# A hybrid decoder layer on one core: the gating unit's two projections as one with 512 columns, and 128 bytes more ahead of two groups of tiles

## The chip, the core and the metric

The kernel runs on one core of one Trainium2 chip. It uses the five engines: PE (TensorE, matrix products; PEld is its weight load), DVE (VectorE), ACT (ScalarE), POOL (GpSimd) and SP (SyncE, which issues the DMAs). The metric is device time in microseconds from launch to end, median over runs.

## The reference, cut to what matters

One layer, 1024 tokens of width 1024, float32. The part that the change touches is the fourth of four mixers, a gating unit over chunks of 128 tokens:

```python
h = rmsnorm(x, ln1_g) * (1 + sc1) + sh1
(..., d_u, d_v) = split(h @ w_in, splits, axis=-1)        # 256 columns each
# sgu_mixer(d_u, d_v)
u = gelu(u)
v = layernorm(gelu(v), ln_g, ln_b)                        # over the 256 columns
sv = einsum('gts,bnsge->bntge', w_causal, v.chunks(128)) + b_s
o_d = u * sv
mix = concat([o_a, o_b, o_c, o_d]) @ w_out
x = x + g1 * mix
x = x + g2 * conv_ffn(rmsnorm(x, ln2_g) * (1 + sc2) + sh2, ffn_up, ..., ffn_down)
```

Ahead of `w_out` stand a convolution with a LayerNorm (`o_a`), gated linear attention (`o_b`) and a dilated attention (`o_c`); `conv_ffn` is an up-projection to 5632 columns, a causal convolution of width 3 and a down-projection from 2816.

## The kernel before, in words

Every float32 product is made of three products with operands rounded to a shorter format. A tile is split into a high part (`ac.copy`, line 70) and a low part (a subtraction on POOL or DVE, line 71), and low times high, high times low and high times high are added up in PSUM (lines 92 to 94, and 1221 to 1223 in the second half of the kernel). The activations of the first half stand in 32 tiles `h` of 128x512 (high and low, by 8 slices of the width and 2 token halves).

The first half goes stage by stage: `first` and `proj_feat` and `proj_tok` project `h` onto groups of columns of `w_in`, one after the other. `weave(main, (gen, rate), ...)` advances the generators of the other mixers some steps at each step of the main projection: attention (`att`), convolution norm (`cn`), linear attention (`lin`), the sums for the later modulations (`ada`, line 828 on DVE) and the splits of finished mixers (`sp`). The tile framework then orders the instructions of each engine by a simulated time line; each engine runs its own in order.

Weights come through `W1`: one tile `wf` (two buffers) is loaded by SP, and split into two tiles `wh` (four buffers, so two pairs) by ACT and POOL. `get` takes the next pair, `refill` splits the next tile when a pair has been used up.

The gating unit's stage is the last of the first half. It projects `d_v` with `proj_tok` (all 8 token tiles, 4 PSUM banks held, matmuls with 256 columns, lines 410 to 412) and then `d_u` with `proj_tok_halves` (two banks for each token half, both weight pairs kept; lines 434 to 436). Its tails `d_v` and `d_u` evict the banks with a GELU of 128x512 (lines 537 and 562), take mean and variance on DVE (line 545), normalize on DVE (550), scale and shift on POOL over 128x1024 (553 and 554), mix tokens on PE (572), combine on DVE (576), transpose on PE (582) and split. Then `out_proj(0)` multiplies the first token half by `w_out`, in the order of slices `KORD = ((0, 1), (4, 5), (6, 7), (2, 3))`, where 6 and 7 are the gating unit's, and `out_proj(1)` the second half.

The second half of the kernel is the feed-forward: 22 steps `f` of the up-projection with 7 products each (`SEQ`), each of 12 matmuls, then 77 steps of the down-projection with 12 matmuls each. For the products P5, P6 and P7 the moving operand (the one with 512 columns) stands in tiles `ht`; for P1 to P4 in tiles `h`. In the down-projection the stationary operand (128 columns at a time) stands in `ht` for every step. The raw tiles that DMAs fill and DVE splits are named `m4` (seen as `m_t` in rows).

Where tiles stand: within each partition the tile pools follow one another. Tiles `x1` (4096 bytes) start at byte 19456, `wf` and `wh` (4352 bytes) at 52224 and 60928, `h` (2048 bytes) at 78336: all multiples of 256. The pool of the second half, `ph2`, starts at 143872, also a multiple of 256, with two kinds of small tiles (`rs_v`, `rs_t`) that take 128 bytes; so the seven tiles `m4` (4096 bytes) start from 144000 and the 24 tiles `ht` (2048 bytes) from 172672, which are multiples of 128 and not of 256.

## Time and profile before

| | us |
|---|---|
| median of 3 runs (1168.76 to 1171.06) | 1170.57 |
| the profiled execution | 1173.14 |
| its span, first to last instruction | 1171.4 |
| PE busy in it | 1120.8 |

Of the profiled execution's time 1171.4 us are the span and 1.7 us lie around it. It is 2.6 us above the median of the runs. A row of busy times counts an instruction from its start to its end; matmuls overlap, so the distance from one start to the next, not the duration, is what a matmul costs in a stream.

### The profile page before, as it was taken

What the parts mean: (1) busy time and instruction counts of PE and PEld (TensorE: products, weight loads), DVE (VectorE), ACT (ScalarE), POOL (GpSimd) and SP (SyncE); (2) the same over time, 40 slices, a digit from 0 to 9 for tenths busy, and PEclk for the clock granted to TensorE, in tenths of its full rate; (3) what the DMA queues carried; (4) which work ended last, traced back from release to release, by engine and by line L of the source; (5) the groups of instructions that cost most, each with busy time, mean ns of one, the idle gap of its engine ahead of it and who ended that gap; (6) DMA issues with size and microseconds to landing.
All of it is one profiled execution on the core that took longest, in us unless ns stands there. A gap on an engine that the chain in (4) does not pass through costs nothing.

```text
span 1171.4 us, 16065 instructions
## 1 busy us (share of the span) xinstructions
PE 1120.8 (96%) x5686; PEld 917.0 (78%) x5686; DVE 810.9 (69%) x1321; ACT 561.8 (48%) x909; POOL 707.6 (60%) x487
## 2 busy tenths in 40 slices
PE   4889999999999999999999999999999999999996
PEld 4668987866797878877887888888887778888885
DVE  6998979376678865555576676857686766654547
ACT  5552235373331523367666555555554646443432
POOL 2565574221232346648978777867787737895963
PEclk9999999989999999999999999999999999999998
DMA  9632232031331534482134546445644488574533
GB/s 354 253 100 71 75 112 86 19 108 58 123 109 64 188 99 180 153 293 76 46 135 135 189 180 242 172 168 183 242 181 178 144 308 329 194 239 142 198 109 144
DMA packets 70145, 186.86 MB, mean 160 GB/s; under 512 B 8097, under 2 KB 9265, under 8 KB 70065
## 3 DMA queue, kind: packets, MB, share of 16 engines
q1 hardware_dynamic: 70064, 185.84, 45.3%
q8 instruction: 45, 0.74, 0.2%
q14 instruction: 36, 0.29, 0.1%
HBM read 141.50 MB, written 42.21 MB: 157 GB/s over the span
## 4 chain that ended last, share of the span: by engine, by line
PE 71%; DVE 6%; POOL 2%; issue 2%; ACT 2%; DMA 2%; SPq 0%; ACTq 0%; DVEq 0%; POOLq 0%
PE a_ps L1221 8%; PE a_ps L1223 8%; PE a_ps L1222 8%; PE s_ps L92 4%; PE s_ps L93 4%; PE s_ps L94 3%; PE e_ps L1221 3%; PE e_ps L1222 3%; PE e_ps L1223 3%; PE y_ps L1223 3%; PE y_ps L1222 3%; PE y_ps L1221 3%; PE c_ps L1223 2%; PE c_ps L1221 2%; PE c_ps L1222 2%
## 5 line engine op out<-in xcount | busy, mean ns | idle before, releaser
L71 POOL TENSOR_TENSOR wh_t<-wf_t,wh_t 128x512 fp32r<-128x512 f32 (+2 forms) x131 | 216.4, 1659 | 178.6 <-ACT wh_t L70 169.3
L70 ACT CAST wh_t<-wf_t 128x512 fp32r<-128x512 f32 (+2 forms) x135 | 98.0, 739 | 139.7 <-PE s_ps L93 35.1
L1114 DVE SCALAR_TENSOR_TENSOR y_ps<-x_t,col,y_ps 128x1023 f32<-128x1023 f32 x88 | 112.6, 1283 | 38.9 <-ACT y_ps L1112 38.1
L71 POOL TENSOR_TENSOR h_t<-m_t,h_t 128x512 fp32r<-128x512 f32 x70 | 102.3, 1476 | 39.2 <-ACT h_t L70 37.3
L71 DVE TENSOR_TENSOR ht_t<-m_t,ht_t 128x512 fp32r<-128x512 f32 x65 | 80.1, 1245 | 65.3 <-ACT ht_t L70 63.5
L1387 ACT COPY x_t<-a_ps 128x512 f32<-128x512 f32 x81 | 47.4, 585 | 79.5 <-PE a_ps L1223 79.4
L471 DVE SCALAR_TENSOR_TENSOR s_ps<-m_t,col,s_ps 128x512 f32<-128x512 f32 (+19 forms) x116 | 80.3, 740 | 1.1
L70 ACT CAST ht_t<-m_t 128x512 fp32r<-128x512 f32 x65 | 40.3, 620 | 78.2 <-DMA m_t<-ps 20.7
L71 POOL TENSOR_TENSOR wh_t<-m_t,wh_t 128x512 fp32r<-128x512 f32 x52 | 67.2, 1305 | 16.5 <-ACT wh_t L70 16.1
L1221 PE MATMUL a_ps<-h_t,wh_t 128*128 128x512 f32 x188 | 73.7, 392 | 1.7 <-ACT x_t L1240 1.0
L828 DVE SCALAR_TENSOR_TENSOR acc<-ad,cond,acc 128x256 f32<-128x256 f32 x112 | 68.8, 622 | 8.8 <-DMA ad<-in_ada 7.3
L1223 PE MATMUL a_ps<-h_t,wh_t 128*128 128x512 f32 x188 | 73.3, 390 | 0.0
L1222 PE MATMUL a_ps<-h_t,wh_t 128*128 128x512 f32 x188 | 73.3, 390 | 0.0
L680 POOL TENSOR_TENSOR m_t<-m_t,mx 128x128 f32<-128x128 f32 (+7 forms) x16 | 19.3, 1206 | 85.2 <-DVE mx L678 82.9
L1221 PE MATMUL a_ps<-ht_t,wh_t 128*128 128x512 f32 x176 | 69.5, 395 | 0.0
L1223 PE MATMUL a_ps<-ht_t,wh_t 128*128 128x512 f32 x176 | 69.5, 395 | 0.0
L1222 PE MATMUL a_ps<-ht_t,wh_t 128*128 128x512 f32 x176 | 69.4, 394 | 0.0
L93 PE MATMUL s_ps<-wh_t,h_t 128*128 128x512 f32 (+1 forms) x192 | 69.2, 361 | 0.0
L94 PE MATMUL s_ps<-wh_t,h_t 128*128 128x512 f32 (+1 forms) x192 | 68.9, 359 | 0.0
L92 PE MATMUL s_ps<-wh_t,h_t 128*128 128x512 f32 (+1 forms) x192 | 65.6, 368 | 1.0 <-DVE g1b L837 1.0
L1221 PE MATMUL e_ps<-h_t,wh_t 128*128 128x512 f32 x148 | 57.9, 391 | 0.9 <-POOL wh_t L71 0.9
L1222 PE MATMUL e_ps<-h_t,wh_t 128*128 128x512 f32 x148 | 57.7, 390 | 0.0
(344 smaller groups left out, 3356.5 us busy)
## 6 DMA issues: line engine op xcount, KB each, us to landing
m_t<-in_ffn_up SPq DMA_DIRECT2D x46, 512.0 KB, 4.8
ad<-in_ada SPq DMA_DIRECT2D x64, 256.0 KB, 3.4
ps<-m_t SPq DMA_DIRECT2D x22, 512.0 KB, 7.3
x_t<-in_ffn_down SPq DMA_DIRECT2D x22, 512.0 KB, 6.8
m_t<-ps SPq DMA_DIRECT2D x33, 256.0 KB, 4.3
x_t<-in_x SPq DMA_DIRECT2D x16, 512.0 KB, 6.3
wf_t<-in_w_out SPq DMA_DIRECT2D x16, 512.0 KB, 3.6
m_t<-in_ffn_down SPq DMA_DIRECT2D x28, 256.0 KB, 5.4
```

The costliest lines, as they stand in the source:

```text
L70: ac.copy(dst_h, src)
L71: return eng.tensor_tensor(dst_l, src, dst_h.bitcast(F32), op=ALU.subtract)
L92: pe.matmul(ps, ll, rh, start=first, stop=False)
L93: pe.matmul(ps, lh, rl, start=False, stop=False)
L94: return pe.matmul(ps, lh, rh, start=False, stop=last)
L471: ve.scalar_tensor_tensor(yA[t][:, o + a:e] if last else y[:, a:], h[:, o + a - s:e - s], cc(O_CW + (CONV_K - 1 - s) * 2 + t), y[:, a:], o ...
L828: ve.scalar_tensor_tensor(acc, f[:, kk, :], cond[:, k:k + 1], acc, op0=ALU.mult, op1=ALU.add)
L1114: ve.scalar_tensor_tensor(y[:, n:], z[:, :S - n], cc(O_FW + 88 - 44 * n + f), y[:, n:], op0=ALU.mult, op1=ALU.add)
L1221: pe.matmul(ps, ll, rh, start=start, stop=False, skip_group_check=True)
L1222: pe.matmul(ps, lh, rl, start=False, stop=False, skip_group_check=True)
L1223: return pe.matmul(ps, lh, rh, start=False, stop=stop, skip_group_check=True)
L1387: ac.copy(dict(P1=lo(za[f]), P6=hi(za[f]), P7=hi(zb), P4=lo(zb))[p], ba)
```

## The change

1. `w_in`'s columns of `d_u` and `d_v` lie side by side; the host now packs them as four tiles `w_uv` of two slices by 512 columns. `proj_gating` replaces both projections: for each token half, four banks, and for each of the four weight tiles 24 matmuls with 512 columns (2 slices x 4 token tiles x 3). The weight tiles are loaded and split once for each token half: eight loads and splits in place of four.
2. `d_uv` takes the place of `d_v` and `d_u`: for each token tile two GELUs of 128x256 and the statistics, and after the fourth tile of a half the rest of the chain, for v and u in one.
3. A tile of 32 float32 that nothing reads or writes is taken from `ph2` ahead of its other tiles, so that `m4` starts at 144128 and `ht` at 172800, both multiples of 256.

```diff
@@ -33,7 +33,7 @@
 C_CQ, C_CK, C_CV = 1296, 1552, 1808
 C_DU, C_DV = 2064, 2320
 FEAT_COLS = (C_AG + P, C_CQ, C_CK, C_CQ + P, C_CK + P, C_BQ, C_BK)
-TOK_COLS = (C_DV, C_DU, C_CV, C_BV)
+TOK_COLS = (C_CV, C_BV)
 
 
 O_C, O_L1, O_L2, O_CG, O_CB, O_VB, O_GB, O_SB, O_AB = 0, 8, 16, 24, 26, 28, 30, 31, 35
@@ -44,7 +44,7 @@
 
 
 @with_exitstack
-def trunk(ctx, tc, x, cols, ada_1, ada_2, ada_b, w_a, w_feat, w_tok, w_glr, gla_w2, gla_norm_g,
+def trunk(ctx, tc, x, cols, ada_1, ada_2, ada_b, w_a, w_feat, w_tok, w_uv, w_glr, gla_w2, gla_norm_g,
           sgu_ln_g, sgu_ln_b, sgu_wt, w_out, ffn_up, ffn_down, lnf_g,
           rope_cos, rope_sin, dil_mask, gla_mask, head_mask, out):
     nc = tc.nc
@@ -225,9 +225,9 @@
         mac_last[:] = [r.ins]
 
     W1 = Weights([(w_a[k], 1024) for k in range(4)] + [(w_feat[FEAT_COLS.index(C_AG + P)], 1024)]
-                 + [(w_feat[1], 1024), (w_feat[2], 1024), (w_tok[2, 0], 1024), (w_tok[2, 1], 1024), (w_feat[3], 1024), (w_feat[4], 1024)]
-                 + [(w_glr[0], 1088), (w_glr[1], 1088), (w_tok[3, 0], 1024), (w_tok[3, 1], 1024), (w_feat[5], 1024), (w_feat[6], 1024)]
-                 + [(w_tok[0, 0], 1024), (w_tok[0, 1], 1024), (w_tok[1, 0], 1024), (w_tok[1, 1], 1024)])
+                 + [(w_feat[1], 1024), (w_feat[2], 1024), (w_tok[0, 0], 1024), (w_tok[0, 1], 1024), (w_feat[3], 1024), (w_feat[4], 1024)]
+                 + [(w_glr[0], 1088), (w_glr[1], 1088), (w_tok[1, 0], 1024), (w_tok[1, 1], 1024), (w_feat[5], 1024), (w_feat[6], 1024)]
+                 + [(w_uv[a], 1024) for _ in range(2) for a in range(4)])
 
     for i in range(4):
         x_load(i)
@@ -416,27 +416,22 @@
                     spawn(W1.refill())
                 yield 1
 
-    def proj_tok_halves(done):
-        ws = [W1.get(), W1.get()]
+    def proj_gating(done):
         for g in range(2):
-            pss = [p_s() for _ in range(2)]
-            for a in range(2):
-                wh, wl = ws[a]
-                for b in range(2):
-                    for i in range(2):
-                        ts = slice((2 * b + i) * P, (2 * b + i + 1) * P)
-                        for kk in range(4):
-                            ks = slice(kk * 256, (kk + 1) * 256)
-                            k = a * 4 + kk
-                            first, last = k == 0 and i == 0, k == KT - 1 and i == 1
-                            out_ = pss[b][:, i * 256:(i + 1) * 256]
-                            lh, ll = hH[k][g][:, ts], hL[k][g][:, ts]
-                            pe.matmul(out_, ll, wh[:, ks], start=first, stop=False, skip_group_check=True)
-                            pe.matmul(out_, lh, wl[:, ks], start=False, stop=False, skip_group_check=True)
-                            pe.matmul(out_, lh, wh[:, ks], start=False, stop=last, skip_group_check=True)
-                    if a == 1:
-                        spawn(done(2 * g + b, pss[b]))
-                    yield 1
+            pss = [p_s() for _ in range(4)]
+            for a in range(4):
+                wh, wl = W1.get()
+                for i in range(4):
+                    ts = slice(i * P, (i + 1) * P)
+                    for kk in range(2):
+                        k = 2 * a + kk
+                        mm3(pss[i], hH[k][g][:, ts], hL[k][g][:, ts], wh[:, half(kk)], wl[:, half(kk)], k == 0, k == KT - 1)
+                    if a == 3:
+                        spawn(d_uv(4 * g + i, pss[i]))
+                    if i % 2:
+                        if i == 3:
+                            spawn(W1.refill())
+                        yield 1
 
     def chain(*gens):
         for g in gens:
@@ -526,24 +521,27 @@
     sy.dma_start(lgb[:, 1, :], sgu_ln_b.rearrange("a b -> (a b)").partition_broadcast(P))
     sy.dma_start(wT, sgu_wt)
     gp.affine_select(out=wT, in_=wT, pattern=[[0, 4], [1, P]], compare_op=ALU.is_ge, fill=0.0, base=0, channel_multiplier=-1)
-    vD, uD = [], []
-
-    def d_v(b, ps):
-        if b == 0:
-            vD.extend([t_x(), t_x()])
-        q = b // 2
-        v = vD[q]
-        yield 1
-        ac.activation(v[:, half(b % 2)], ps, AF.Gelu_apprx_tanh)
-        if b % 2 == 0:
+    vD, uD, mvs = [], [], {}
+
+    def d_uv(t, ps):
+        q, i = t // 4, t % 4
+        if i == 0:
+            vD.append(t_x())
+            uD.append(t_x())
+        v, u = vD[q], uD[q]
+        yield 1
+        for w, c0 in ((v, 256), (u, 0)):
+            ac.activation(w[:, i * 256:(i + 1) * 256], ps[:, c0:c0 + 256], AF.Gelu_apprx_tanh)
+        if i == 0:
+            mvs[q] = sm1.tile([P, 4, 2], F32, tag="mvD", name="mvD", bufs=2)
+        mv = mvs[q]
+        st = sm1.tile([P, 6], F32, tag="bn", name="bn", bufs=2)
+        ve.bn_stats(st, v[:, i * 256:(i + 1) * 256])
+        ve.bn_aggr(mv[:, i, :], st)
+        if i < 3:
             return
         yield 1
-        mv = sm1.tile([P, 4, 2], F32, tag="mvD", name="mvD", bufs=2)
         rs = sm1.tile([P, 4], F32, tag="rsD", name="rsD", bufs=2)
-        for i in range(4):
-            st = sm1.tile([P, 6], F32, tag="bn", name="bn", bufs=2)
-            ve.bn_stats(st, v[:, i * 256:(i + 1) * 256])
-            ve.bn_aggr(mv[:, i, :], st)
         rsqrt(rs, mv[:, :, 1], [P, 4], 1.0, sm1)
         for i in range(4):
             vv = v[:, i * 256:(i + 1) * 256]
@@ -552,18 +550,8 @@
         v3 = v.rearrange("p (i n) -> p i n", i=4)
         gp.tensor_tensor(v3, v3, lgb[:, 0:1, :].broadcast_to([P, 4, 256]), op=ALU.mult)
         gp.tensor_tensor(v3, v3, lgb[:, 1:2, :].broadcast_to([P, 4, 256]), op=ALU.add)
-
-    def d_u(b, ps):
-        if b == 0:
-            uD.extend([t_x(), t_x()])
-        q = b // 2
-        u = uD[q]
-        yield 1
-        ac.activation(u[:, half(b % 2)], ps, AF.Gelu_apprx_tanh)
-        if b % 2 == 0:
-            return
+        yield 1
         u3 = u.rearrange("p (i n) -> p i n", i=4)
-        v3 = vD[q].rearrange("p (i n) -> p i n", i=4)
         svs = []
         for g2 in range(2):
             sv = p_s()
@@ -983,7 +971,7 @@
     cn = delay(2, chain(conv_norm(), silus()))
     lin = delay(16, linear())
     sp = delay(6, splits([(kt, 0) for kt in (4, 5, 0, 1)]))
-    weave(chain(proj_tok(d_v), proj_tok_halves(d_u)), (att, 1.45), (cn, 1.05),
+    weave(proj_gating(d_uv), (att, 1.45), (cn, 1.05),
           (lin, 2.43), (ada, 2.08), (sp, 0.97))
     flush(att, cn, sp)
     while "g1" not in have:
@@ -1246,6 +1234,7 @@
 
 
     raw, tok = {}, {}
+    ph2.tile([P, 32], F32, name="pad")
 
     def token_rows(n):
 
@@ -1543,6 +1532,7 @@
     r['w_a'] = w[:, :, 0:512].reshape(4, 2, P, 512).transpose(0, 2, 1, 3).reshape(4, P, 1024)
     r['w_feat'] = np.stack([w[:, :, c:c + P].transpose(1, 0, 2).reshape(P, 1024) for c in FEAT_COLS])
     r['w_tok'] = np.stack([w[:, :, c:c + 256].reshape(2, 4, P, 256).transpose(0, 2, 1, 3).reshape(2, P, 1024) for c in TOK_COLS])
+    r['w_uv'] = w[:, :, C_DU:C_DU + 512].reshape(4, 2, P, 512).transpose(0, 2, 1, 3).reshape(4, P, 1024)
     r['w_glr'] = w[:, :, C_BG:C_BG + 272].reshape(2, 4, P, 272).transpose(0, 2, 1, 3).reshape(2, P, 1088)
     r['gla_w2'] = a['gla_w2'][0]
     r['gla_norm_g'] = a['gla_norm_g']
```

## Rows read from the trace of the kernel before

**Rows 1.** The page, busy us by engine over the span.

```profile
PE 1120.8 (96%) x5686; PEld 917.0 (78%) x5686; DVE 810.9 (69%) x1321; ACT 561.8 (48%) x909; POOL 707.6 (60%) x487
```

**Rows 2.** Windows: length, busy us by engine, clock granted, DMA share, GB/s.

```profile
core 0: us, PE busy (x) PEld busy (x) DVE busy (x) ACT busy (x) POOL busy (x), PEclk, DMA share, GB/s
...
345.00:365.00 20.00, 17.21 (x114) 14.92 (x113) 19.51 (x39) 5.20 (x13) 10.85 (x6) 0.91 0.18 53
365.00:385.00 20.00, 20.00 (x151) 18.27 (x151) 16.46 (x43) 4.75 (x8) 4.85 (x2) 1.00 0.32 106
385.00:400.00 15.00, 12.50 (x93) 11.08 (x92) 11.84 (x32) 10.82 (x16) 3.64 (x2) 0.89 0.87 314
400.00:440.00 40.00, 40.00 (x191) 30.40 (x191) 28.13 (x45) 11.07 (x22) 19.45 (x11) 1.00 0.23 73
...
640.00:880.00 240.00, 240.00 (x1046) 196.13 (x1045) 170.66 (x183) 129.57 (x187) 184.63 (x138) 1.00 0.53 191
960.00:1120.00 160.00, 160.00 (x691) 129.70 (x690) 91.29 (x89) 72.96 (x132) 122.59 (x84) 1.00 0.65 221
```

**Rows 3.** The same view, for instructions that read or write `ht` tiles alone.

```profile
0.00:1172.00 1172.00, 419.35 (x1764) 331.23 (x1764) 112.45 (x97) 58.56 (x97) 2.59 (x2) 0.99 0.46 159
```

**Rows 4.** Timeline of PE in the up-projection: start us, duration us, line, operands.

```profile
733.69 0.40 PE L1222 MATMUL a_ps<-ht_t,wh_t 128*128 128x512 f32 x1
...
737.19 0.39 PE L1223 MATMUL c_ps<-ht_t,wh_t 128*128 128x512 f32 x1
...
744.32 0.39 PE L1221 MATMUL a_ps<-h_t,wh_t 128*128 128x512 f32 x1
...
749.31 0.39 PE L1221 MATMUL a_ps<-h_t,wh_t 128*128 128x512 f32 x1
```

**Rows 5.** Timeline of PE in the down-projection.

```profile
1049.79 0.39 PE L1221 MATMUL y_ps<-h_t,ht_t 128*128 128x512 f32 x1
...
1052.81 0.39 PE L1222 MATMUL y_ps<-h_t,ht_t 128*128 128x512 f32 x1
```

**Rows 6.** Timeline of PE in the projection with 272 columns.

```profile
167.80 0.28 PE L93 MATMUL s_ps<-wh_t,h_t 128*128 128x272 f32 x1
...
170.57 0.29 PE L94 MATMUL s_ps<-wh_t,h_t 128*128 128x272 f32 x1
```

**Rows 7.** Timeline of PE in the gating unit's projection.

```profile
316.94 0.28 PE L410 MATMUL s_ps<-wh_t,h_t 128*128 128x256 f32 x1
...
323.30 0.28 PE L412 MATMUL s_ps<-wh_t,h_t 128*128 128x256 f32 x1
```

**Rows 8.** Groups by line and shape, 311 to 412 us: busy, mean ns, idle before.

```profile
L71 POOL TENSOR_TENSOR wh_t<-wf_t,wh_t 128x1024 fp32r<-128x1024 f32 x5 | 11.9, 2383 | 39.1 <-ACT wh_t L70 34.4 <-DMA ad<-in_ada 4.7
L70 ACT CAST wh_t<-wf_t 128x1024 fp32r<-128x1024 f32 x5 | 5.2, 1050 | 19.9 <-PE s_ps L435 8.7 <-PE s_ps L411 6.7 <-issue 4.5
L537 ACT ACTIVATE x_t<-s_ps 128x512 f32<-128x512 f32 x4 | 2.4, 596 | 5.6 <-PE s_ps L412 5.6
```

**Rows 9.** Timeline of ACT: an eviction of 256 columns.

```profile
356.34 0.37 ACT L929 COPY m_t<-s_ps 128x256 f32<-128x256 f32 x1 [3.69 <-PE s_ps L926]
```

**Rows 10.** Timelines of DVE and of POOL around the statistics of the second half.

```profile
345.36 2.03 DVE L77 TENSOR_SCALAR rs_v<-mvD 128x4 f32<-128x4 f32 x1
347.42 0.17 DVE L78 TENSOR_SCALAR rsD<-rs_v 128x4 int32<-128x4 int32 x1
347.62 2.23 DVE L80 TENSOR_TENSOR rs_t<-rsD 128x4 f32<-128x4 f32 x1
...
344.97 2.39 POOL L553 TENSOR_TENSOR x_t<-x_t,m_t 128x1024 f32<-128x1024 f32 x1
347.44 2.39 POOL L554 TENSOR_TENSOR x_t<-x_t,m_t 128x1024 f32<-128x1024 f32 x1
```

**Rows 11.** The chain that ended last, 386 to 401 us: start, us, what.

```profile
388.48 3.31 DVE m_t L948
391.80 0.60 DVE h_t L71
392.40 1.58 DVE x_t L576 x4
...
396.91 3.02 PE s_ps L888 x32
```

**Rows 12.** DMA issues by tensor: count, KB each, median us to landing.

```profile
wf_t<-in_w_tok SPq DMA_DIRECT2D x8, 512.0 KB, 3.5
```

## The prediction

> **What bounds the kernel now.** I read the page first: PE is busy 1120.8 of 1171.4 us [rows 1], so almost everything that shortens PE's stream shortens the kernel, and the question is stage by stage how long a matmul takes and who makes PE wait. The windows answer the second part [rows 2]: from 640 to 880 us (up-projection) and from 960 to 1120 us (down-projection) PE is never idle, while DVE, ACT and POOL are busy at most 77% of the time. In the gating unit's stage, 312 to 400 us, PE stands still in two places, 2.79 us in the window from 345 and 2.50 us in the one from 385, and in both DVE is the fullest other engine (19.51 of 20 us in the first). So two stretches must be told apart: the second half of the kernel, where PE alone sets the end, and the gating stage, where PE and DVE take turns.
>
> Then the timeline of PE, for the distance between starts. It shows that matmuls of one shape do not all cost the same. In the up-projection, 23 matmuls whose operands stand in `h` and `wh` start 226.6 ns apart (744.32 to 749.31, 22 steps), and 16 whose moving operand stands in `ht` start 233.3 ns apart (733.69 to 737.19, 15 steps) [rows 4]. In the down-projection, where the stationary operand stands in `ht`, 14 matmuls start 232.3 ns apart [rows 5]. The two kinds alternate within microseconds in the same stage, at the same clock of 1.00, so it is a property of the tiles. `ht` tiles differ from `h` and `wh` in two ways that I know of: they start at an odd multiple of 128 bytes, and they lie higher in the partition. In all 1764 matmuls touch `ht` [rows 3].
>
> **The padding tile.** It adds no instruction and moves `ht` and `m4` by 128 bytes. If the start address is what costs the time, the 1764 matmuls fall to 226.6 ns. Down-projection: 924 matmuls (77 steps x 12) by 232.3 - 226.6 = 5.7 ns is 5.3 us; by the window's mean (160 us / 691 = 231.5 ns) it is 4.5 us. Up-projection: the other 840 by 233.3 - 226.6 = 6.7 ns is 5.6 us; the window's mean (240 us / 1046 = 229.4 ns, three sevenths of it the slow kind) gives 2.8 x 7/3 = 6.5 ns and 5.5 us. Together 10.0 to 10.9 us; I take 10. A few of these stand at stage ends where PE waits for others, and POOL, busy 77% in the up-projection [rows 2], has room to follow a PE that is 1.3% faster. The lower bound is nothing.
>
> Why I believe it: the penalty appears for a moving and for a stationary operand alike, and the start address is what both have in common. One row speaks neither way: in the projection with 272 columns the slices of `wh` start 0, 64, 128 and 192 bytes off a multiple of 256, and 23 of its matmuls start an even 125.8 ns apart [rows 6], about what its width asks for beside 120.0 ns for 256 columns [rows 7]. But 1088 bytes touch five blocks of 256 bytes from any of these starts, whereas 2048 bytes touch eight when aligned and nine when not, and 512 bytes two or three. A cost for each block touched would fit all four observations; that is my guess, not a thing the rows show.
>
> [...]
>
> `m4` tiles are filled by DMA and read by ACT, POOL and DVE. In the windows of the second half PE waits for none of these, so I count that part as nothing; if loads or splits were slower or faster by a few per cent, PE's full windows would hide it.
>
> **The projection with 512 columns.** Removed: 2 x 192 matmuls with 256 columns at 120.0 ns (317 to 323 us, 53 steps [rows 7]), 46.1 us. Added: 192 with 512 columns at 226.6 ns, 43.5 us; both operands are in `wh` and `h`. PE gains 2.6 us.
>
> Added beside it: four more weight tiles. Each is a load on SP's queue (3.5 us to landing [rows 12]; behind it in that queue stand the loads for the modulation sums, which nobody needs before the second norm), a cast on ACT (1.05 us) and a subtraction on POOL (2.38 us) [rows 8]. ACT: 4 x 1.05 us, and 16 GELUs of 256 columns (0.37 us by the nearest eviction of that size [rows 9]) for 8 of 0.60 us [rows 8] is 1.1 us; 5.3 us more for an engine with over 10 us idle in every 20 up to 385 us [rows 2]: nothing. POOL: 9.5 us more, with about 9 of 20 us idle at worst [rows 2]. In itself nothing, but POOL holds DVE up. At 344.97 and 347.44 us POOL scales and shifts; DVE's two instructions on 4 columns in the same moments last 2.03 and 2.23 us in place of 0.17 and end when POOL's end [rows 10]. So a POOL pass can cost DVE up to its own 2.38 us. [...]
>
> What is it worth here? Four passes cost DVE between nothing and 9.5 us; the first idle place of PE is where DVE is full, so about half may reach PE. Against it, the second token half's statistics, scaling and combining (about 6 us of DVE with the waits of [rows 10]) move behind the projection's end, where DVE is busy only 28 of 40 us and PE is full [rows 2]. They delay slices 6 and 7 of the second token half, which `out_proj(1)` needs only after `out_proj(0)`, 192 matmuls or 43.5 us later: that is the cover. The handover itself, with its 2.50 us of idle PE, hangs on DVE's L948 (3.31 us) and the combining behind it [rows 11], and a PE that is done earlier waits there longer. And four banks instead of two are held in the second part, which leaves four for the other mixers. [...] The stage then gains 2.6 - 1.6 = 1 us.
>
> **The sum.** 10 + 1 = 11 us. The profiled execution took 1173.14 us, 1171.4 of them span, and would take 1162.1; it lies 2.6 us above the median of the runs, so the median goes from 1170.57 to 1159.6, say 1160 us. Differences below 0.2% (2.3 us) can hardly be told from no change.
>
> **The rivals.**
>
> *The loss eats most of the gain.* The padding pays 10 us, but each of the four added subtractions holds DVE for its full length and PE with it: -2.6 + 9.5 = +7 us for the stage, 1170.6 - 10 + 7 = 1167.6 us. For it: DVE is at 19.51 of 20 us from 345 us. Against it: two of the four windows leave DVE room, and the moved chain relieves it.
>
> *The start address is not the reason.* `ht` is slow because of where it lies, or the unread tile is not laid out at all. Then only the stage's 1 us remains: 1169.6 us, no change. For it: no row shows an aligned tile as high as `ht` in a stream of this shape, and the 272 columns do not mind their starts. Against it: the regular 6 ns for both kinds of operand.
>
> *Slower.* POOL's passes become the stage's clock: besides the four subtractions, the two passes of the second half (2.39 us each) now fall at the handover, where DVE's L948 to L576 end the chain [rows 10, 11]. If all six hold DVE on the path, 6 x 2.39 = 14.3 us, and PE falls to the lower clock at two more places (some 1.7 us each, as a window of 15 us at 0.89 has lost), that is 17.7 - 2.6 = 15.1 us for the stage, and the padding's 10 us leave +5: 1175.7 us. It decides once the six passes cost PE more than 14.9 us. Against it: in [rows 10] only two passes in succession hit DVE, and behind 400 us PE has work that needs neither.
>
> **How the numbers follow.** The forecast has 0.66 (1156 to 1164.5 us by the bounds of the padding and a loss of 0 to 4 us), the eaten gain 0.14 (1165 to 1169.5), the wrong reason 0.10 (1168 to 1172), slower 0.10. Faster by over 0.2% means below 1168.2 us: all of the first, most of the second and a tenth of the third, 0.76. Within 0.2%: the rest of the second and most of the third, 0.13. Slower: 0.11. The range from 1155 to 1169 us holds the first, nearly all of the second and a little of the third, a good 8 in 10.
>
> **What would show it.** Right: starts of matmuls with `ht` operands 226 to 227 ns apart; the two full windows' matmuls per us up to 4.41; the gating matmuls about 227 ns apart and 192 of them; PE's idle time between 312 and 400 us no more than 2 us above 5.3. Wrong: `ht` matmuls still at 232 ns; long DVE instructions beside POOL's added subtractions with PE idle behind them; PE waiting for `wh` of the output projection between 400 and 415 us; or POOL setting the pace of the up-projection once PE is faster.

## The result: 0.7% slower, and the profile after

The changed kernel takes 1178.47 us (median of 5 runs, 1177.74 to 1183.62) where the kernel before takes 1170.47 beside it (1168.76 to 1171.06): a ratio of 1.0068, 95% interval 1.0044 to 1.0091. The forecast was 1160 us and a range to 1169, so both the range and the direction were wrong. The profiled execution took 1177.74 us, 1176.0 of them span.

The stages, each from the start of its first matmul in PE's timeline to the start of the next one's (up- and down-projection share their lines and run into each other; the border between them is counted back from the last matmul and good to half a microsecond, its differences between runs to 0.3 us):

| us | before | after | forecast for the difference | measured |
|---|---|---|---|---|
| start to first gating matmul | 311.7 | 310.1 | 0 | -1.6 |
| gating matmuls and handover, to first `out_proj` matmul | 88.2 | 98.3 | -1 | +10.1 |
| output projection | 106.9 | 106.9 | 0 | 0.0 |
| up-projection | 438.7 | 439.7 | -5.5 | +1.0 |
| down-projection, to last matmul | 214.9 | 209.7 | -4.5 to -5.3 | -5.2 |
| after it | 11.0 | 11.4 | 0 | +0.4 |

One of three terms came out as forecast. The differences add up to those of the profiled spans, 4.6 us, and not to the medians' 8.0 us: the profiled execution of before lay 2.6 us above its median, that of after 0.7 us below. The page's busy times answer to [rows 1]: PE's busy time is 12.7 us less and the span is 4.6 us longer.

```profile
PE 1108.1 (94%) x5494; PEld 905.1 (77%) x5494; DVE 823.0 (70%) x1321; ACT 565.3 (48%) x921; POOL 723.3 (62%) x491
```

The windows (columns as in [rows 2]) say where. The down-projection is full and denser, 708 matmuls where there were 691. The up-projection, full before, has 4.3 us of idle PE between 640 and 880 us. And between 385 and 400 us PE does next to nothing, at a mean granted clock of 0.58: it is 1.00 up to 387.2 us and 0.50 from 387.4 on; PE had stood still since 383.0. When it comes back it is still granted 0.50 (from 400 to 403 us).

```profile
core 0: us, PE busy (x) PEld busy (x) DVE busy (x) ACT busy (x) POOL busy (x), PEclk, DMA share, GB/s
640.00:880.00 240.00, 235.66 (x1038) 194.24 (x1037) 166.84 (x175) 127.86 (x187) 185.99 (x137) 1.00 0.52 186
960.00:1120.00 160.00, 160.00 (x708) 132.48 (x707) 97.14 (x93) 74.45 (x133) 119.91 (x81) 1.00 0.66 228
...
345.00:365.00 20.00, 18.88 (x100) 14.99 (x101) 17.98 (x34) 5.84 (x13) 7.71 (x4) 1.00 0.31 101
365.00:385.00 20.00, 17.69 (x94) 14.11 (x92) 19.98 (x47) 9.64 (x19) 9.27 (x4) 1.00 0.55 183
385.00:400.00 15.00, 0.80 (x2) 0.71 (x3) 9.50 (x38) 3.80 (x5) 7.45 (x3) 0.58 0.37 141
400.00:403.00 3.00, 3.00 (x9) 2.27 (x9) 0.88 (x2) 0.00 (x0) 0.00 (x0) 0.50 0.00 0
```

The padding did to each matmul what was forecast. In PE's timeline (columns as in [rows 4]) 12 matmuls with their moving operand in `ht` start 226.4 ns apart (11 steps) in the up-projection, and 16 with the stationary operand there 226.7 ns apart (15 steps) in the down-projection, against 233.3 and 232.3 in [rows 4, 5].

```profile
738.95 0.39 PE L1209 MATMUL a_ps<-ht_t,wh_t 128*128 128x512 f32 x1
...
741.44 0.39 PE L1211 MATMUL a_ps<-ht_t,wh_t 128*128 128x512 f32 x1
...
1049.48 0.39 PE L1210 MATMUL y_ps<-h_t,ht_t 128*128 128x512 f32 x1
...
1052.88 0.39 PE L1210 MATMUL y_ps<-h_t,ht_t 128*128 128x512 f32 x1
```

The gating projection did its part too: its last matmul starts at 380.8 us, 6.2 us earlier than before (387.0), of which 1.6 us come from an earlier first one. (The expectation of E4 below reckons with 7.3 us.) What follows is the loss. PE's waits between 370 and 415 us (who waited for whom: us in total, times, longest):

```profile
PE s_ps L560 <- POOL x_t L552: 16.2, 1, 16.2
```

L560 are the mixing matmuls of the second token half. In the chain that ended last they close a run of dependent steps: the reciprocal root on DVE, the normalizing L548, POOL's two passes, the mixing.

```profile
388.98 1.20 DVE rsD L82
...
391.75 1.06 DVE x_t L548 x3
392.88 3.86 POOL x_t L551
396.81 2.35 POOL x_t L552
399.20 3.79 PE s_ps L560 x8
```

None of this is needed by `out_proj(0)`. Its first operands, slices 0 and 1 of the first half, were split at 390.2 us by POOL and at 394.5 by DVE (the timelines of both), and its first matmul starts at 408.4, because L560, the transposes L570 and L944, and L876 and L885 stand ahead of it in PE's queue. So PE's order alone accounts for the time from 394.5 us on; from 383.0 to 394.5, 11.5 of the 16.2 us, it would have waited in this order of slices whatever stood in its queue.

```profile
388.89 1.26 POOL L71 TENSOR_TENSOR h_t<-m_t,h_t 128x512 fp32r<-128x512 f32 x1 [4.34 <-ACT h_t L70]
...
393.85 0.69 DVE L71 TENSOR_TENSOR h_t<-m_t,h_t 128x512 fp32r<-128x512 f32 x1
```

No matmul of `out_proj` went ahead of those in front of it in PE's queue: the first ones, ready at 394.5 us, started at 408.4.

### The profile page after: what moved, and what is told of

Read it like the earlier page. It is cut to its first block, busy times and chain, and to the rows that moved or that the text cites. A ratio compares the mean times of both kernels' runs of the same rounds, so it can differ in the third digit from the quotient of the medians.

```text
span 1176.0 us, 15719 instructions
## 1 busy us (share of the span) xinstructions
PE 1108.1 (94%) x5494; PEld 905.1 (77%) x5494; DVE 823.0 (70%) x1321; ACT 565.3 (48%) x921; POOL 723.3 (62%) x491
## 4 chain that ended last, share of the span: by engine, by line
PE 62%; DVE 8%; POOL 4%; issue 4%; DMA 4%; ACT 3%; SPq 0%; ACTq 0%; POOLq 0%; DVEq 0%
PE a_ps L1209 7%; PE a_ps L1211 7%; PE a_ps L1210 7%; PE s_ps L92 4%; PE s_ps L93 4%; PE s_ps L94 4%; PE e_ps L1209 3%; PE e_ps L1210 3%; PE y_ps L1211 3%; PE y_ps L1210 3%; PE y_ps L1209 3%; PE e_ps L1211 3%; POOL wh_t L71 2%; DMA x_t<-in_ffn_down 2%; PE c_ps L1211 2%
## 5 line engine op out<-in xcount | busy, mean ns | idle before, releaser
L71 POOL TENSOR_TENSOR wh_t<-wf_t,wh_t 128x512 fp32r<-128x512 f32 (+2 forms) x135 | 226.4, 1687 | 154.4 <-ACT wh_t L70 139.5
L70 ACT CAST wh_t<-wf_t 128x512 fp32r<-128x512 f32 (+2 forms) x139 | 101.5, 747 | 132.1 <-PE s_ps L93 37.6
L71 DVE TENSOR_TENSOR ht_t<-m_t,ht_t 128x512 fp32r<-128x512 f32 x65 | 82.7, 1287 | 56.8 <-ACT ht_t L70 56.4
L93 PE MATMUL s_ps<-wh_t,h_t 128*128 128x512 f32 (+1 forms) x256 | 94.7, 370 | 0.0
L94 PE MATMUL s_ps<-wh_t,h_t 128*128 128x512 f32 (+1 forms) x256 | 94.4, 369 | 0.0
L92 PE MATMUL s_ps<-wh_t,h_t 128*128 128x512 f32 (+1 forms) x256 | 91.4, 379 | 1.4 <-DVE g1b L825 1.4
L816 DVE SCALAR_TENSOR_TENSOR acc<-ad,cond,acc 128x256 f32<-128x256 f32 x112 | 77.1, 691 | 8.0 <-DMA ad<-in_ada 6.3
```

The lines of the kernel that those rows point to most:

```text
L70: ac.copy(dst_h, src)
L71: return eng.tensor_tensor(dst_l, src, dst_h.bitcast(F32), op=ALU.subtract)
L92: pe.matmul(ps, ll, rh, start=first, stop=False)
L93: pe.matmul(ps, lh, rl, start=False, stop=False)
L94: return pe.matmul(ps, lh, rh, start=False, stop=last)
L816: ve.scalar_tensor_tensor(acc, f[:, kk, :], cond[:, k:k + 1], acc, op0=ALU.mult, op1=ALU.add)
```

## The experiments

Each kernel was timed beside the kernel before on the same chip; the median of before lay between 1170.9 and 1172.2 us. Stages are measured as in the table above, and "PE idle" is the sum of the gaps of over 0.25 us between matmuls in PE's timeline of that stage.

### The two parts alone, and PE's queue

E1 adds the one line of the padding to the kernel before; E2 takes it out of the changed kernel.

```diff
     raw, tok = {}, {}
+    ph2.tile([P, 32], F32, name="pad")
```

> The kernel before with the 128-byte tile and nothing else. Theory A (padding pays in both stages, the loss is all in the gating stage): 1170.5 - 10 = 1160.5 us, up-projection about 5 us shorter and down-projection 5.2 us shorter. Theory B (in the up-projection the faster matmuls only wait longer for split weights, as the trace of the changed kernel shows it with +1.0 us for that stage): about 1165.5 us, with 5.2 us gained in the down-projection alone and waits on `wh` behind POOL in the up-projection. Rival (the start address is not what counts): 1170 us, ht matmuls still 232 to 233 ns apart.

> The changed kernel without the padding tile. If the handover loses 10 us whatever the padding does, this is 1170.5 + 10 = 1180 us or, if the padding is worth only its 5.2 us of the down-projection, 1178.5 + 5 = 1183.5 us. First out_proj matmul some 8 to 10 us later than before, PE idle about 16 us ahead of it. If the loss came from the padding (its gating stage is untouched by it), this would be near 1170 us.

E3 hands the second half's mixing to PE inside `out_proj(0)`, and E4 is E3 without the padding.

```diff
         gp.tensor_tensor(v3, v3, lgb[:, 1:2, :].broadcast_to([P, 4, 256]), op=ALU.add)
+        if q:
+            return
         yield 1
+        yield from d_mix(q)
+
+    def d_mix(q):
...
-    weave(out_proj(0), (lin, 0.59), (sp, 0.7), (ada, 2.2))
+    mix = delay(4, d_mix(1))
+    weave(out_proj(0), (lin, 0.59), (sp, 0.7), (ada, 2.2), (mix, 0.75))
```

> The changed kernel with one thing moved: the second token half's mixing matmuls, combining and transposes are handed to PE among the matmuls of out_proj(0) instead of ahead of it. Theory (PE's queue order at the handover is the loss): out_proj(0) starts about 10 us or more earlier than 408.4 us, near 395 us when its first slices are split; PE's 16 us of idle time ahead of it falls to some 3 to 6 us; 1165 to 1169 us. Rival 1 (four more POOL splits and two POOL passes hold DVE, so the operands themselves are late): start stays within 3 us of 408 us and the time stays near 1176 us. Rival 2 (the second half's chain is merely moved and now delays out_proj(1)): out_proj(0) starts early but the up-projection still starts near 515 us.

> The same move without the padding tile: with e3 it gives the worth of the padding once more. Theory A: 10 us above e3; theory B: 5 us above e3. Against the kernel before it gives the projection with 512 columns by itself, order mended: the projection ended 7.3 us earlier in the changed kernel, so 1163 to 1168 us if all of that reaches the end, about 1170 us if the handover keeps it.

| | median us | ratio (95%) | first gating to first up-projection matmul | up-projection | down-projection |
|---|---|---|---|---|---|
| before | 1171.06 | | 195.1 | 438.7 | 214.9 |
| E1 padding alone | 1167.60 | 0.9965 (0.9949 to 0.9982) | 194.7 | 441.1 | 209.8 |
| E2 gating alone | 1183.01 | 1.0110 (1.0080 to 1.0139) | 204.5 | 439.3 | 214.9 |
| E3 mixing held | 1176.18 | 1.0032 (1.0013 to 1.0050) | 203.3 | 438.6 | 209.7 |
| E4 held, no padding | 1182.65 | 1.0097 (1.0071 to 1.0123) | 203.4 | 440.1 | 214.9 |

E1 and E2 separate the two losses cleanly. The gating change costs 9.4 us in its stage without the padding (E2 against before) and 10.4 with it (after against E1). The padding gains its 5.1 us in the down-projection and nothing in the up-projection, which becomes 2.4 us longer although its matmuls are faster: theory B. E4 lies 6.5 us above E3, nearer to theory B's 5 than to A's 10, and 11.6 us above the kernel before, outside both of its figures for the 512 columns alone. E3 hardly helped: `out_proj(0)` starts 7.7 us earlier, at 400.7, but the stage is only 1.8 us shorter. PE now waits for the next item of its queue, the linear attention's norm, which itself stands behind the second half's chain on DVE:

```profile
PE s_ps L950 <- DVE m_t L942: 11.0, 1, 11.0
```

### Is DVE, or POOL, simply too full there?

From the first gating matmul to 400 us the sums on L816 (the L828 of before) and POOL's weight splits show these groups in the changed kernel (busy us, mean ns); before, 41 sums took 20.8 us, 528 ns each, and 4 splits 9.5 us.

```profile
L816 DVE SCALAR_TENSOR_TENSOR acc<-ad,cond,acc 128x256 f32<-128x256 f32 x41 | 28.8, 710 | 5.4 <-DMA ad<-in_ada 4.9
...
L71 POOL TENSOR_TENSOR wh_t<-wf_t,wh_t 128x1024 fp32r<-128x1024 f32 x8 | 19.6, 2450 | 22.2 <-ACT wh_t L70 12.7 <-issue 9.6
```

The sums grew by 8 us, as the prediction's "slower" rival has it. By the timelines of DVE and POOL the 29 of the 41 sums beside which POOL did nothing last 0.48 us in the mean, as 36 do before; the 12 that meet a POOL instruction last 1.27 us (5 before, 0.91 us). E5 takes the added loads and splits away (the second token half then has only two of its four weight tiles), E6 puts their subtraction on DVE, E7 moves sums out of the stage.

```diff
@@ E5
+        ws = []
...
-                wh, wl = W1.get()
+                if g == 0:
+                    ws.append(W1.get())
+                wh, wl = ws[a] if g == 0 else ws[2 + a % 2]
@@ E6
-                split(h[:, :n], l[:, :n], f[:, :n], gp)
+                split(h[:, :n], l[:, :n], f[:, :n], ve if i >= len(self.srcs) - 4 else gp)
@@ E7
-          (lin, 2.43), (ada, 2.08), (sp, 0.97))
+          (lin, 2.43), (ada, 1.0), (sp, 0.97))
-    weave(out_proj(0), (lin, 0.59), (sp, 0.7), (ada, 2.2))
+    weave(out_proj(0), (lin, 0.59), (sp, 0.7), (ada, 3.3))
```

> The changed kernel without the second loading and splitting of the gating weights: the second token half multiplies by the last two weight tiles, still in place, instead of all four, so that half of the gating unit's output is left uncomputed in its proper form; the number and shape of matmuls stay. Theory P (DVE bounds the stage, and POOL's added passes hold it: DVE's 195 instructions from the first gating matmul to the first out_proj matmul last 92.2 us in the changed kernel, 193 last 82.9 us before): the sums on L822 fall from 0.71 us to some 0.55 us each, DVE's total by 6 to 9 us, out_proj(0) starts 6 to 9 us earlier, 1170 to 1172 us. Rival (the second half's chain of statistics, scaling and mixing ends late whatever POOL does): DVE's total may fall, but PE still stands still for 14 to 16 us ahead of out_proj(0) and the time stays within 2 us of 1178.5.

> The changed kernel with the subtractions of the second token half's four weight tiles on DVE instead of POOL (about 1.2 us each by the 128x1024 rows of DVE, where POOL takes 2.4). Theory P, with POOL's passes costing DVE their own length: DVE saves 4 x 2.4 and pays 4 x 1.2, 4 to 5 us earlier, 1174 us. Rival (holding costs DVE little, its work was simply moved to the end): DVE pays 4.8 us more and the kernel takes 1180 to 1183 us.

> The changed kernel with the sums for the later modulations (L822) advanced 1.0 instead of 2.08 steps for each step of the gating projection, and 3.3 instead of 2.2 in out_proj(0), where DVE is busy 21 of 30 and 33 of 60 us. Theory P (DVE is the bound from 325 to 395 us): some 20 of the 41 sums leave the stage, 0.5 to 0.7 us each, 10 us or more of DVE; out_proj(0) starts up to 8 us earlier and 1169 to 1172 us are left, unless out_proj pays. Rival (POOL's own chain sets the handover): no more than 2 us.

| | median us | ratio (95%) | gating to up-projection | PE idle in it |
|---|---|---|---|---|
| after | 1178.47 | 1.0068 (1.0044 to 1.0091) | 205.1 | 17.6 |
| E5 no second loading | 1175.87 | 1.0041 (1.0024 to 1.0058) | 203.4 | 16.4 |
| E6 splits on DVE | 1179.03 | 1.0067 (1.0046 to 1.0088) | 204.9 | 18.0 |
| E7 sums later | 1189.26 | 1.0157 (1.0131 to 1.0182) | 214.3 | 23.5 |

Theory P falls. E5 takes four splits from POOL, and the sums fall only from 28.8 to 26.3 us for 41 (649 ns each, 528 before with as many splits): taking the added splits away gives back 2.5 of the 8 us. By both timelines 5 of E5's sums still meet a weight split, 5 in the changed kernel and 3 before: where the passes fall beside the sums counts, more than how many there are. PE still waits 15.8 us for the same pass of POOL (L555 there). E5's 2.6 us below the changed kernel lie within the two intervals. E6 is within 1 us of the changed kernel. E7, with 14 sums fewer ahead of `out_proj(0)` (27 for 41), starts it no earlier (98.6 us after the first gating matmul, 98.3 in the changed kernel) and is 11 us slower, because its output projection takes 115.7 us in place of 106.9: there PE waits 5.0 us for the sums moved into it, and the clock granted is 0.78 from 440 to 450 us and 0.71 from 450 to 460, 5 us of work lost. So neither engine's load sets the handover; what is late is a chain. E5's group of sums, and its wait:

```profile
L819 DVE SCALAR_TENSOR_TENSOR acc<-ad,cond,acc 128x256 f32<-128x256 f32 x41 | 26.3, 649 | 5.4 <-DMA ad<-in_ada 4.9
```

```profile
PE s_ps L563 <- POOL x_t L555: 15.8, 1, 15.8
```

And E7's wait in the output projection:

```profile
PE s_ps L828 <- DVE acc L816: 5.0, 1, 5.0
```

### The order of the handover, mended

E15 begins `out_proj(0)` with the attention's slices 4 and 5 (the weights are packed in that order), ahead of the convolution norm's and the linear attention's last steps. E16 traces the second half's chain from its rsqrt on inside `out_proj(0)`. E10 does both. (The last line is E10's; E16 has `out_proj(0)` in place of `op0`.)

```diff
@@ E15, E10
-    KORD = ((0, 1), (4, 5), (6, 7), (2, 3))
+    KORD = ((4, 5), (0, 1), (6, 7), (2, 3))
...
+    op0 = out_proj(0)
+    for _ in range(2):
+        next(op0)
+        step()
+    flush(cn, splits([(0, 0), (1, 0)]))
@@ E16, E10
-        if i < 3:
-            return
-        yield 1
+        if i == 3 and q == 0:
+            yield 1
+            yield from d_tail(q)
+
+    def d_tail(q):
...
+    tail = delay(2, d_tail(1))
+    weave(op0, (lin, 0.59), (sp, 0.7), (ada, 2.2), (tail, 1))
```

> The changed kernel with the handover in another order: out_proj(0) begins with the attention's slices 4 and 5, split long before, and its first 24 matmuls stand in PE's queue ahead of the linear attention's norm; the second token half's chain of the gating unit, from its statistics' rsqrt on, is traced inside out_proj(0). Theory Q (what was lost is the order of the queues at the handover, DVE's and PE's both): PE's 16.5 us without work fall to 3 to 6 us, and the 17 us of half clock around them to 3 to 7 us; the stretch from first gating to first up-projection matmul falls from 205 us to 193 to 196 us; 1167 to 1170 us. Rival P2 (the operands are late because DVE is full from 325 to 395 us, in any order): the idle time moves behind the first 24 matmuls, and the stretch stays above 200 us; 1174 us or more.

> The changed kernel with out_proj(0) beginning with slices 4 and 5 and traced ahead of the convolution norm's second half and the linear attention's norm, but with the second token half's chain of the gating unit traced where it was. In PE's queue 71 of out_proj's matmuls now stand ahead of that chain's mixing matmuls. If PE's order alone was the loss: 1167 to 1169 us as with both changes (1167.8). If the chain's place on DVE and POOL counts too: 1171 to 1174 us.

> The changed kernel with the second token half's chain traced inside out_proj(0) from its rsqrt on, but out_proj(0) still beginning with slices 0 and 1 and behind the linear attention's norm. PE can start out_proj(0) when slices 0 and 1 are split and the norm's transposes are done: DVE reaches the norm a little earlier without L548 ahead of it (1.4 us), POOL splits without L551 and L552 (5 to 6 us). Expected 1172 to 1175 us, PE idle 9 to 11 us ahead of out_proj(0); if the chain on DVE and POOL was the loss, 1168 us.

| | median us | ratio (95%) | gating to up-projection | PE idle in it |
|---|---|---|---|---|
| E15 slices 4 and 5 first | 1177.55 | 1.0059 (1.0042 to 1.0075) | 204.8 | 12.9 |
| E16 chain held | 1176.90 | 1.0043 (1.0027 to 1.0060) | 201.6 | 11.1 |
| E10 both | 1167.77 | 0.9968 (0.9954 to 0.9981) | 193.7 | 5.6 |

Theory Q holds, but only for both together, which I had not expected to be so sharp: alone they return 1 and 2 us, within the intervals and less than any of their expectations, together 11. (One sign of E10 missed: PE is at a lower granted clock for longer than the 3 to 7 us expected, at 0.50 from 393 to 403 us.) PE's waits show why. In E15, with the chain still on DVE, PE starts `out_proj` at 382.0 us and then waits for a split and for sums behind the chain:

```profile
PE s_ps L92 <- DVE h_t L71: 6.1, 1, 6.1
PE s_ps L828 <- DVE acc L816: 4.2, 1, 4.2
```

The two orders work against each other there: the chain's combining stands at the head of DVE's queue, and its mixing behind 71 matmuls of `out_proj(0)` in PE's, so DVE stands still:

```profile
408.38 1.74 DVE L564 SCALAR_TENSOR_TENSOR x_t<-s_ps,col,x_t 128x256 f32<-128x256 f32 x4 [14.40 <-PE s_ps L560]
```

In E16, with PE's queue as it was, the norm's transposes wait for DVE:

```profile
PE s_ps L947 <- DVE rs_t L81: 9.1, 1, 9.1
```

E16 is hardly more than E3: `out_proj(0)` starts at 400.8 us, there at 400.7, and DVE still runs the chain's rsqrt among the norm's steps from 390 to 395 us. So whether E10 needs the chain's place on DVE and POOL, or only E3's later mixing on PE beside the new order of slices, was not tested. In E10 one shorter wait is left:

```profile
PE s_ps L947 <- DVE m_t L939: 3.6, 1, 3.6
```

### Where the padding's gain in the up-projection went

In E1 PE waits for POOL's split of a weight tile 5.1 us in 3 places (0.9 in one before). One of them, followed back through POOL, ACT and DVE (timelines of E1; in brackets the idle time before an instruction and what ended it):

```profile
885.14 1.22 DVE L1157 TENSOR_TENSOR x_t<-x_t 128x512 f32<-128x512 f32 x1 [5.88 <-DMA x_t<-in_ffn_down]
...
894.49 1.22 DVE L1125 TENSOR_TENSOR y_ps<-x_t,y_ps 128x1024 f32<-128x1024 f32 x1
...
895.74 1.01 ACT L1127 COPY x_t<-y_ps 128x1024 f32<-128x1024 f32 x1 [7.44 <-DVE y_ps L1125]
896.65 0.62 ACT L70 CAST wh_t<-m_t 128x512 fp32r<-128x512 f32 x1
...
897.35 1.27 POOL L71 TENSOR_TENSOR wh_t<-m_t,wh_t 128x512 fp32r<-128x512 f32 x1 [4.74 <-ACT wh_t L70]
```

And at its end PE's wait between 890 and 905 us:

```profile
PE e_ps L1221 <- POOL wh_t L71: 2.9, 1, 2.9
```

The same waits stand in the trace of before, between 600 and 925 us, where PE hardly feels them:

```profile
DVE x_t L1157 <- DMA x_t<-in_ffn_down: 35.3, 10, 5.0
ACT x_t L1127 <- DVE y_ps L1125: 24.2, 13, 5.5
PE e_ps L1221 <- POOL wh_t L71: 0.9, 1, 0.9
```

DVE's sums for the down-projection (`weight_sums`, L1157 on) wait for their load; the product L1125 stands behind them, ACT's copy waits for the product, the weight cast stands behind the copy, and POOL and PE come last. E8 traced the sums two steps later, E9 queues the first of them behind the product; both have the padding. E13 is E9 without the padding, E17 is E9's edit on the changed kernel. E14 is E1 with 256 bytes.

```diff
@@ E8
+        yield 1
+        yield 1
@@ E9, E11, E12, E13, E17
+        yield 1
+        yield 1
-        ve.tensor_tensor(lo(we), hi(we), lo(we), op=ALU.subtract)
+        with tc.issue_after(prods[-1]):
+            ve.tensor_tensor(lo(we), hi(we), lo(we), op=ALU.subtract)
@@ E14
+    ph2.tile([P, 64], F32, name="pad")
```

> The kernel before with the padding tile, and in the up-projection two steps more between the loads of weight_sums and its first DVE instruction. Theory W (with faster matmuls the up-projection waits for DVE: it waits for the load of weight_sums, 38 us in 10 places, ACT's copy L1127 waits for DVE's product behind it, 43 us, the weight cast stands behind that copy, POOL's split behind the cast): PE's waits from 600 to 920 us fall from some 7 us with pad alone to 1 us, no spell of half clock there, up-projection 4 to 5 us shorter than with pad alone: 1162.5 us. Rival (POOL is simply too slow for the faster PE): the waits stay, 1166 to 1168 us.

> The kernel before with the padding tile, and DVE's four sums of weight_sums put behind the product of the same step (L1125) in DVE's queue, instead of ahead of it, where they wait for their load 36 to 38 us in 10 places. Theory W (the up-projection loses the padding's gain to this wait, by way of ACT's copy, the weight cast behind it and POOL's split): ACT's wait for that product falls from 43 us to under 20, PE's stalls from 600 to 920 us from some 7 us to 2 us and their half clock with them, up-projection 4 to 5 us shorter than with pad alone (441 to 436 us): 1162 to 1163 us. Rival (POOL is too slow for the faster PE): stalls as with pad alone, 1166 to 1168 us.

> The kernel before with the sums of weight_sums behind the product and without the padding tile: with the first of the earlier four (both: 1156.3 us) it gives the padding's worth where the up-projection no longer waits. Theory W (the padding's gain of 5.5 us in the up-projection was real and eaten by that wait): 1156.3 + 10 to 11 = 1166 to 1167.5 us, ht matmuls 232 to 233 ns apart. Rival (the sums' place is worth all of it, the padding only its 5.2 us of the down-projection): 1161 to 1162 us.

> The kernel before with an unused tile of 256 bytes instead of 128: `m4` and `ht` lie higher, but still start at odd multiples of 128 bytes. If the start address is what counts, nothing changes: 1170 to 1172 us, matmuls with ht operands 232 to 233 ns apart. If any shift of these tiles did it (where they lie, what they lie beside), 226 to 227 ns and 1166 to 1168 us as with 128 bytes.

> The changed kernel with the sums of weight_sums behind the product and nothing else. If the two losses are independent (about 10 us at the handover, some 11 us in the up-projection), this is 1178.5 - 11 = 1167 to 1168 us, with the first gating to first up-projection matmul still 204 to 205 us apart and the up-projection 429 us. If the late handover and the waits in the up-projection hang together, the up-projection stays above 433 us or the time below 1160 us.

| | median us | ratio (95%) | up-projection | PE idle in it |
|---|---|---|---|---|
| before | 1171.06 | | 438.7 | 5.4 |
| E1 padding | 1167.60 | 0.9965 (0.9949 to 0.9982) | 441.1 | 9.2 |
| E8 padding, sums two steps later | 1166.54 | 0.9974 (0.9952 to 0.9995) | 443.4 | 11.4 |
| E13 sums behind | 1170.47 | 0.9991 (0.9981 to 1.0001) | 437.3 | 3.5 |
| E9 padding, sums behind | 1156.26 | 0.9871 (0.9850 to 0.9891) | 428.8 | 2.3 |
| E14 256 bytes | 1171.33 | 1.0008 (0.9993 to 1.0023) | 437.8 | 3.9 |
| E17 changed kernel, sums behind | 1167.89 | 0.9961 (0.9943 to 0.9978) | 429.0 | 2.6 |

E8 changed nothing that counts: DVE still waits 36.9 us in 10 places for those loads, so it is E1 measured again (its profiled execution lay 8 us above its median, so the two columns on the right say little). E9 goes past its forecast: 11 us below E1 where some 5 were expected. The windows from 850 us to the end of the stage show both halves of the loss, idle time and clock. In E1 7.4 us of 94.7 are without work, at a mean granted clock of 0.96. Two of its four stalls are followed by a spell at a lower granted clock; each of the two stretches of 6 us around them was granted 0.72, so 3.4 us of work are lost:

```profile
898.00:904.00 6.00, 5.33 (x16) 4.26 (x17) 3.07 (x3) 3.44 (x6) 4.59 (x5) 0.72 0.57 193
932.00:938.00 6.00, 5.17 (x16) 3.80 (x16) 4.75 (x7) 1.53 (x2) 1.28 (x1) 0.72 0.26 87
850.00:944.70 94.70, 87.30 (x373) 70.47 (x373) 65.15 (x67) 51.87 (x79) 68.73 (x56) 0.96 0.51 181
```

In E9 it is 0.9 us of 83.6, at 1.00:

```profile
850.00:933.60 83.60, 82.73 (x373) 68.66 (x372) 59.26 (x68) 49.30 (x76) 67.71 (x54) 1.00 0.63 221
```

The account of E1's up-projection nearly closes on these: -5.5 us of spacing (the forecast's figure), +3.8 of idle time (9.2 - 5.4), +3.4 of clock, together +1.7 for +2.4 measured. The forecast for E9 had taken the loss as the missing gain alone; the idle time and the clock that E1 adds went too. E13 was a miss: the sums' place is worth next to nothing by itself, which makes the padding's worth beside it larger than expected (1170.5 where 1166 to 1167.5 was forecast); PE waits for no split for longer than 0.3 us there, and in the trace of before for 0.9 us at most. Padding and sums are worth 3.5 and 0.4 us alone and 14.8 together.

E14 settles what about the tile counts. With 256 bytes `ht` lies higher and still starts at an odd multiple of 128: 14 matmuls of the down-projection start 232.3 ns apart (13 steps), as in [rows 5], and the time is that of before.

```profile
1060.07 0.40 PE L1221 MATMUL y_ps<-h_t,ht_t 128*128 128x512 f32 x1
...
1063.09 0.39 PE L1222 MATMUL y_ps<-h_t,ht_t 128*128 128x512 f32 x1
```

E17 came out within its 1167 to 1168 us, with the up-projection at 429.0 us: the two losses add up. Its profiled execution, 3.0 us above its median, shows 207.8 us from the first gating to the first up-projection matmul where 204 to 205 were expected.

### Both mended, with and without the 512 columns

E11 is E10 with the sums behind the product; E12 is the kernel before with the padding, the sums behind the product and E15's order of slices.

> The one before with the sums of weight_sums behind the product too: both mends on the changed kernel. Theories Q and W together: 1162 to 1165 us; if only one of the two holds, 1167 to 1170 us or 1173 us.

> The kernel before with the padding tile, the sums behind the product and out_proj(0) beginning with slices 4 and 5 ahead of the linear attention's norm, the gating unit projected as before. Against the first of these four it gives the worth of that order without the 512 columns: PE stood still only 2.7 us at this handover, so 0 to 4 us, 1159 to 1163 us. If the 512 columns are worth their 2.6 us once the handover's order is mended, the version with both projections as one is 1 to 3 us below this; if they cost more on DVE and POOL than they save on PE, it lies above.

| | median us | ratio (95%) | gating to up-projection | up-projection |
|---|---|---|---|---|
| E11 512 columns | 1155.44 | 0.9865 (0.9843 to 0.9888) | 192.8 | 429.0 |
| E12 256 columns | 1154.86 | 0.9856 (0.9835 to 0.9876) | 193.8 | 428.1 |

E11 did better than its 1162 to 1165 us and E12 than its 1159 to 1163, as E9 had. Both beat both kernels by 1.3% and more. Between them lies nothing that the measurement can tell: with the handover mended the 512 columns give 1.0 us in their stage, within the spread of the profiles. (E12 has E15's order of slices alone, E11 has the chain moved as well.)

## Why the prediction was wrong

- *"A property of the tiles", the padding's mechanism*: right. 226.4 to 226.7 ns with `ht` aligned, 232.3 with it 256 bytes further (E14). The rival that the address is not the reason is out. A cost for each block of 256 bytes touched is my guess from [rows 4 to 7]; E14 agrees with it, and no run tested it beyond that.
- *Down-projection, 5.3 us (4.5 by the window's mean)*: right, 5.2.
- *Up-projection, 5.5 us; "POOL, busy 77%, has room to follow a PE that is 1.3% faster"*: this step failed. Its size was right (E9 against E13: the up-projection is 8.5 us shorter, of which idle time and clock explain 2.9 and spacing the rest), its condition was not met: in E1 the stage came out 2.4 us longer. POOL had room in the mean; the cast that it waited for stood behind a copy that waited for DVE, and DVE for a load. These waits were in the trace of before, 35 us for DVE's loads and 24 us for ACT's copy, and cost PE 0.9 us there. I read the busy shares and did not follow the chain that feeds PE.
- *"They delay slices 6 and 7 of the second token half, which `out_proj(1)` needs only after `out_proj(0)`: that is the cover"*: this is the step that turned the sign. The result is indeed not needed for 43.5 us. But the instructions that make it stand ahead of `out_proj(0)` in PE's queue and, in DVE's, ahead of a split that `out_proj(0)` begins with, and PE stood still for 16.2 us at an instruction that nobody was waiting for. The stage was forecast at -1 and came at +10.1; with the queues' order mended (E10, E11) it is -1.4 to -2.3. The new order gives E12, with the 256 columns, -1.3, so the 512 columns' own share is 0 to -1.
- *The price of four more splits, "between nothing and 9.5 us"*: on the end it was little: E5 without them is 2.6 us faster, and its stage 1.7 us shorter. On DVE the sums grew by 8 us, but only 2.5 of them go when the added splits go (E5). No run shows the 1.6 us that the sum takes off the 2.6 for all that comes with the 512 columns: the stage became 10.1 us longer with them, and 1.4 to 2.3 us shorter with the queues' order mended (E10, E11).
- *The "slower" rival* had the right sign and place (1175.7 us) and a mechanism that the runs do not bear out: POOL's passes holding DVE. E5 takes four of its six passes away, and of 17.6 us of idle time 16.4 stay. The other two, L551 and L552, are in the chain with 3.86 and 2.35 us, as work that PE itself waits for.
- *What would show it*: the line "PE's idle time between 312 and 400 us no more than 2 us above 5.3" told against the forecast at first sight, with 17.6.

Not tested: which engine's share of the moved chain E10 needs beside the new order of slices.

## What to carry to other kernels

A chain that is moved costs what it holds up in every queue in which its instructions stand (here 16.2 us of PE at L560), and "needed only later" covers nothing while they stand ahead of work that is needed now. Giving PE other work first and moving the chain were each worth 1 to 2 us here (E15, E16), both together 11. Before counting a faster matmul as time, follow the waits of the engines that feed PE back to their first cause, even where they cost PE nothing yet: the padding was worth 3.5 us, and 14.8 with one wait taken out of its way. Where matmuls of one shape come at two distances in one stage (here 226.6 and 233.3 ns), look at the start address of the operands' tiles modulo 256 bytes.

## What the runs showed of the hardware

A matmul with 512 columns of this type took 5.6 to 6.9 ns more when the tile of its moving or stationary operand started at an odd multiple of 128 bytes (232.3 to 233.3 ns against 226.4 to 226.7), and a shift by 256 bytes changed nothing. In the changed kernel's gating stage DVE's sums of 128x256 took 0.48 us each where POOL did nothing beside them and 1.27 us where they met one of its instructions; over all of them 0.53 us before, with 4 weight splits of POOL in the stretch, 0.71 with 8, and 0.65 in E5, with 4 again but as many sums beside them as with 8. After 16.2 us without matmuls PE came back at a granted clock of 0.50, measured from 400 to 403 us. In the last 94.7 us of E1's up-projection, with four stalls of 0.8 to 2.9 us, the mean granted clock was 0.96, against 1.00 in E9 with one of 0.9 us.
